# Two transformer blocks in split fp32: up projections by seven products of quarters, hidden activations through DRAM

## The chip, the core and the metric

The kernel runs on one core of a Trainium2 chip. A core has TensorE (matmuls from SBUF into PSUM), VectorE, ScalarE, GpSimd and SyncE, which work through their own queues in order and wait for each other by semaphores, and 16 DMA engines. The metric is the device time of one execution in microseconds, as the median of the runs.

## What is computed

The reference runs two transformer blocks on one sequence of 1024 tokens with 1024 features. The first has a recurrent (RWKV) and convolutional mixer and a gated feed-forward network, the second has two kinds of attention and a squared-ReLU network. The change touches the two networks:

```python
def _channel_mixer(hn, w_up, ffn_conv_w, ffn_conv_b, w_down):      # D_FF = 2816
    f = jnp.einsum('btd,df->btf', hn, w_up)                        # 1024 -> 2 x 2816
    f = _causal_dwconv(f, ffn_conv_w) + ffn_conv_b                 # 3 taps along the sequence
    gate, up = jnp.split(f, 2, axis=-1)
    return jnp.einsum('btf,fd->btd', jax.nn.gelu(gate) * up, w_down)
...
        u = rms_norm(h, g_mlp[i])
        h = h + jnp.square(jax.nn.relu(u @ w_ff1[i])) @ w_ff2[i]   # 1024 -> 4096 -> 1024
```

## The kernel before, in words

Activations are feature-major: a tile has 128 features on the partitions and one half (`hf`, 512 columns) of the sequence. Every fp32 product is made as three matmuls of a faster type: a value is split into a high part (a cast by ScalarE) and a low part (value minus high part, by VectorE or GpSimd), and hi·hi, hi·lo and lo·hi are summed in PSUM. `load_w` (L126) brings a 512 KB block of weights by SyncE's queue (L133), casts it (L134) and subtracts (L135, on the engine that `split_engine` names); `split` (L124, L125) does the same for activations; `mm3` (L138 on) issues 3 x 8 = 24 matmuls of 512 columns for a block of 128 outputs over 1024 inputs and one half; `dense` does it for both halves. Its PSUM tile `ps_mm` comes from three banks in turn (`PBUFS`, mm=3).

The first network (`GatedUp`) has 22 pairs of a gate block j and an up block 22+j. The result of each product goes through ScalarE (L789: bias and middle tap, out of PSUM), two more taps on VectorE (L790, L792, PSUM and SBUF inputs) and small edge operations between the halves; then gelu (L803), the product of gate and up (L806) and a split into tiles that the down projection reads. The second network (`SquaredUp`) has 32 blocks with relu (L826), square (L827) and split. `Ffn` works in chunks of 4 or 5 hidden blocks (`CH1`, `CH2`): the up blocks of a chunk, then `downs`, which adds the chunk's product into eight accumulators in SBUF (L878 copies the first chunk, L880 adds later ones). In the second network the accumulators start from the residual, loaded from `h_d`. The last chunk is woven by `finish`: up blocks of one half, down of the first half, the rest of the up blocks, down of the second, with the norm that follows (sum of squares on TensorE at L205, squares on ScalarE at L232, their additions on VectorE at L234) under them.

The first part of the kernel, up to the first up blocks of half 0, has its TensorE order written by `weave`, which interleaves threads of work by gaps; outside it a scheduler of the language orders each engine's instructions by estimated costs and free buffers. From L1486 the low parts of weights are made on GpSimd, from L1498 on VectorE again, and from L1521 on GpSimd.

## Time and profile before

| what | value |
|---|---|
| median of 3 runs (lowest, highest) | 3130.33 us (3129.96, 3135.51) |
| the profiled execution | 3127.2 us, of it the span 3125.5 us, granted clock 0.971 |
| TensorE busy | 2993.0 us, 96% of the span, 14752 matmuls |
| VectorE, ScalarE, GpSimd busy | 1650.0, 1157.3, 686.8 us |
| DMA | 294.64 MB, mean 94 GB/s |

The busy share is a mean over phases. The mixer lies at 0 to about 830 us, the first network up to about 1500, attention and its branches up to about 2250, the second network and the gate of the last stage behind it. Granted clock 1.00 is the upper of TensorE's two levels, 2.4 GHz. In rows of matmuls the mean duration overlaps from one matmul to the next, so the time per matmul is read from the stretch divided by the count.

### The profile page before, as it was taken

The numbers are of one execution on the slowest core, as the hardware profiler recorded it, in microseconds if no ns is written. First come the engines' busy times: TensorE is split into PE (matmuls) and PEld (weight loads), VectorE is DVE, ScalarE is ACT, GpSimd is POOL, SyncE is SP. The second block draws the span as 40 slices with busy tenths as digits, with TensorE's granted clock in tenths as the row PEclk, the third lists the DMA queues.
The fourth block names the chain that finished last, engine by engine and source line by source line (L and its number), as shares of the span: only waits on it lengthen the run. The fifth ranks groups of instructions, "written<-read, shape, count | busy, mean of one in ns | idle before, by whom it ended". The sixth has DMA issues, their size and how long they took to land.

```text
span 3125.5 us, 39161 instructions
## 1 busy us (share of the span) xinstructions
PE 2993.0 (96%) x14752; PEld 2392.3 (77%) x14752; DVE 1650.0 (53%) x3180; ACT 1157.3 (37%) x2037; POOL 686.8 (22%) x868
## 2 busy tenths in 40 slices
PE   7969899989999999999999999999999999999997
PEld 5747677777788888888778877768888888888876
DVE  6636454537824444535746755576653333333477
ACT  5433332335533232324445655563341221122343
POOL 2143323501100000025633445550000000000343
PEclk8989898999999999999999999999999999999999
DMA  6543422225421111123532312226542111111233
GB/s 216 176 111 103 125 81 83 80 86 171 122 63 48 41 51 51 38 73 123 174 114 68 90 56 70 65 82 210 179 157 59 40 45 55 43 41 48 81 115 134
DMA packets 164860, 294.64 MB, mean 94 GB/s; under 512 B 56120, under 2 KB 65848, under 8 KB 164672
## 3 DMA queue, kind: packets, MB, share of 16 engines
q1 hardware_dynamic: 132400, 241.77, 25.9%
q10 hardware_dynamic: 32272, 50.38, 4.5%
q8 instruction: 116, 1.90, 0.3%
q14 instruction: 72, 0.59, 0.1%
HBM read 238.31 MB, written 53.77 MB: 93 GB/s over the span
## 4 chain that ended last, share of the span: by engine, by line
PE 47%; DVE 3%; ACT 1%; issue 1%; DMA 0%; POOL 0%; ACTq 0%; DVEq 0%; POOLq 0%
PE ps_mm L143 41%; PE pso L1182 1%; PE pss L1137 1%; DVE sq L234 1%; PE pst L1175 1%; PE pss L1136 1%; DVE xl L125 1%; PE pso L1098 0%; DVE xn L257 0%; PE pst L1093 0%; DVE g L1305 0%; PE ps_sp L205 0%; DMA out<-o 0%; PE pss L1066 0%; DVE o L1313 0%
## 5 line engine op out<-in xcount | busy, mean ns | idle before, releaser
L143 PE MATMUL ps_mm<-xh,wh 128*128 128x512 f32 x2304 | 928.3, 403 | 2.9 <-ACT xh L124 1.5
L143 PE MATMUL ps_mm<-xl,wh 128*128 128x512 f32 x2304 | 924.8, 401 | 1.3 <-DVE xl L125 1.3
L135 POOL TENSOR_TENSOR wl<-wr,wh 128x1024 fp32r<-128x1024 f32 (+2 forms) x133 | 279.7, 2105 | 1733.9 <-ACT wh L134 1521.2
L134 ACT CAST wh<-wr 128x1024 fp32r<-128x1024 f32 (+3 forms) x384 | 354.2, 923 | 726.0 <-PE ps_mm L143 648.1
L143 PE MATMUL ps_mm<-xh,wl 128*128 128x512 f32 x2304 | 612.6, 401 | 0.0
L143 PEld LDWEIGHTS ps_mm<-xh,wh 128*128 128x128 f32 x2304 | 439.3, 191 | 103.0 <-issue 2.2
L143 PEld LDWEIGHTS ps_mm<-xl,wh 128*128 128x128 f32 x2304 | 439.4, 191 | 99.6 <-DVE xl L125 2.5
L143 PEld LDWEIGHTS ps_mm<-xh,wl 128*128 128x128 f32 x2304 | 431.0, 190 | 97.3 <-issue 1.9
L135 DVE TENSOR_TENSOR wl<-wr,wh 128x1024 fp32r<-128x1024 f32 (+2 forms) x251 | 273.2, 1089 | 263.9 <-PE ps_mm L143 217.9
L880 DVE TENSOR_TENSOR acc<-acc,ps_mm 128x512 f32<-128x512 f32 x176 | 120.9, 687 | 304.6 <-PE ps_mm L143 304.6
L143 PE MATMUL ps_mm<-hq,wh 128*128 128x512 f32 x864 | 218.6, 395 | 0.0
L143 PEld LDWEIGHTS ps_mm<-hq,wh 128*128 128x128 f32 x864 | 162.8, 188 | 38.0
L143 PE MATMUL ps_mm<-hh,wh 128*128 128x512 f32 x432 | 170.6, 397 | 1.2 <-ACT wh L134 1.2
L143 PE MATMUL ps_mm<-hl,wh 128*128 128x512 f32 x432 | 170.9, 396 | 0.8 <-DVE hl L125 0.8
L657 POOL TENSOR_TENSOR pr<-mt,lt 128x60 f32<-128x60 f32 (+24 forms) x248 | 88.6, 357 | 331.4 <-DMA lt<-d_l 312.6
L1159 POOL TENSOR_SCALAR S<-S,sm 128x512 f32<-128x512 f32 (+3 forms) x96 | 118.8, 1248 | 98.6 <-DVE sm L1157 70.4
L234 DVE TENSOR_TENSOR sq<-sq 128x512 f32<-128x512 f32 x112 | 108.0, 964 | 34.9 <-ACT sq L232 26.4
L790 DVE SCALAR_TENSOR_TENSOR ft<-ps_mm,vec,ft 128x511 f32<-128x511 f32 x88 | 65.7, 746 | 113.1 <-ACT ft L789 112.9
L143 PE MATMUL ps_mm<-hh,wl 128*128 128x512 f32 x432 | 117.0, 397 | 0.0
L143 PE MATMUL ps_mm<-hq,wl 128*128 128x512 f32 x432 | 116.3, 394 | 0.0
L143 PE MATMUL ps_mm<-yh,wh 128*128 128x512 f32 x256 | 103.9, 407 | 5.1 <-ACT yh L124 5.1
L789 ACT ACTIVATE ft<-ps_mm,vec 128x512 f32<-128x512 f32 x88 | 68.5, 779 | 103.2 <-PE ps_mm L143 102.1
(307 smaller groups left out, 4137.8 us busy)
## 6 DMA issues: line engine op xcount, KB each, us to landing
wr<-in_w_up SPq DMA_DIRECT2D x62, 512.0 KB, 3.6
wr<-in_w_in SPq DMA_DIRECT2D x58, 512.0 KB, 3.9
wr<-in_w_ff SPq DMA_DIRECT2D x41, 512.0 KB, 3.6
wr<-in_w_in2g SPq DMA_DIRECT2D x32, 512.0 KB, 3.6
wr<-in_w_ff SPq DMA_DIRECT2D x32, 320.0 KB, 2.9
wr<-in_w_out SPq DMA_DIRECT2D x16, 512.0 KB, 4.3
wr<-in_w_dn SPq DMA_DIRECT2D x32, 256.0 KB, 2.7
res<-h_d SPq DMA_DIRECT2D x32, 256.0 KB, 4.2
```

The source lines that it names most:

```text
L125: (engine or self.nc.vector).tensor_tensor(out=pair[1], in0=src, in1=pair[0], op=ALU.subtract)
L134: nc.scalar.copy(out=hi, in_=raw)
L135: (engine or self.split_engine).tensor_tensor(out=lo, in0=raw, in1=hi, op=ALU.subtract)
L143: self.nc.tensor.matmul(ps, lhsT=a[:, j, :cols], rhs=x[j][hf][part], start=i == 0, stop=i == 3 * kb - 1)
L234: self.nc.vector.tensor_tensor(out=sq, in0=acc, in1=sq, op=ALU.add)
L657: e.tensor_tensor(out=pr, in0=mt[:, :n, i:i + 1].to_broadcast([128, n, m]), in1=lt[:, i:i + 1, i + 1:].to_broadcast([128, n, m]), op=ALU.mult)
L789: nc.scalar.activation(out=t, in_=ps, func=AF.Identity, bias=k.vc("ffn_conv_b", m), scale=c(2))
L790: nc.vector.scalar_tensor_tensor(out=t[:, 1:], in0=ps[:, :-1], scalar=c(1), in1=t[:, 1:], op0=ALU.mult, op1=ALU.add)
L880: k.nc.vector.tensor_tensor(out=o, in0=o, in1=ps, op=ALU.add)
L1136: nc.tensor.matmul(ps, lhsT=qs[:, e, qc], rhs=kh[e][:, kc], start=True, stop=False)
L1137: nc.tensor.matmul(ps, lhsT=qs[own, e, qc], rhs=kl[0][own, kc], start=False, stop=True)
L1159: nc.gpsimd.tensor_scalar(out=s, in0=s, scalar1=sums[0], scalar2=None, op0=ALU.mult)
```

## The change

Up projections of most blocks are made by a Strassen-Winograd scheme with seven products of quarters in place of eight. The quarters are the two halves of the 1024 inputs (4 row tiles each) times two blocks of weights, and the same halves times the two halves of the sequence. In the first network 17 of 22 pairs (gate j and up 22+j, j from 5) go this way, in the second 13 pairs of neighbouring blocks (from block 6). The first 5 and 6 blocks keep `dense`.

`Quads.operands` makes, once per network, the sums and differences of the input: 16 additions of high and low part on GpSimd, 16 differences T1 to T4 on VectorE, and 16 splits. `Quads.weights` makes for every pair four sums or differences S1 to S4 on GpSimd and splits the two raw blocks' quarters (one split of 1024 columns, five of 512; the low parts of S2 and S3 on GpSimd, the rest on VectorE). `pair` issues 7 x 12 matmuls into three PSUM tiles, two of which gather several products (their partial sums are copied out by ScalarE on the way and added by VectorE). The result of a pair goes through the convolution and gelu, or relu and square, as tiles of 1024 columns in SBUF, and is stored in DRAM (`hid_d`) by ScalarE's queue. After all up blocks the down projections read it back and split it (`hidden`), in chunks of 4, 4, 4, 2, 8 and 4 x 6, 8. `finish` only holds the two halves of the last chunk's down projection. Pools in SBUF are opened and closed by phase.

The diff, cut to the parts spoken of:

```diff
-CH1 = (5, 5, 4, 4, 4)
-CH2 = (5, 5, 5, 5, 4, 4, 4)
-BUFS = dict(am=2, q=10, t=32, nt=5, tp=14, tg=5, tr=1, mt=1, pr=2, wc=4, cd=2, sm=10, mk=1)
+CH1 = (4, 4, 4, 2, 8)
+CH2 = (4, 4, 4, 4, 4, 4, 8)
+WORK = dict(nt=5, tg=5, tp=14, am=2)
+MIX = dict(WORK, q=10, tr=1, mt=1, pr=2, wc=4, mk=1, cd=2)
+ATT = dict(WORK, cd=2, sm=10)
+QUAD = dict(T=24, ws=20, ct=5, tg=4)
...
+    def conv(self, m, t, src):
+        k, nc = self.k, self.k.nc
+        c = lambda i: k.vc("ffn_conv_w", i * 2 * self.nff + m)
+        nc.scalar.activation(out=t, in_=src, func=AF.Identity, bias=k.vc("ffn_conv_b", m), scale=c(2))
+        for i in (1, 2):
+            nc.vector.scalar_tensor_tensor(
+                out=t[:, i:], in0=src[:, :-i], scalar=c(2 - i), in1=t[:, i:], op0=ALU.mult, op1=ALU.add)
...
+    def pairs(self, js):
+        return [((j,), j, self.nff + j) for j in js]
+    def pair(self, js, cs, keep):
+        k, j = self.k, js[0]
+        ts = []
+        for part in (0, 1):
+            t = k.a("ct", [128, 1024], name="ft")
+            self.conv(part * self.nff + j, t, cs[part])
+            if part == 0:
+                k.nc.scalar.activation(out=t, in_=t, func=AF.Gelu_apprx_tanh)
+            ts.append(t)
+        k.nc.vector.tensor_tensor(out=ts[1], in0=ts[0], in1=ts[1], op=ALU.mult)
+        keep(j, ts[1])
...
+    def pairs(self, js):
+        return [((j, j + 1), j, j + 1) for j in js[::2]]
+    def pair(self, js, cs, keep):
+        k = self.k
+        for j, c in zip(js, cs):
+            k.nc.scalar.activation(out=c, in_=c, func=AF.Relu)
+            k.nc.vector.tensor_tensor(out=c, in0=c, in1=c, op=ALU.mult)
+            keep(j, c)
...
+    def operands(self, x):
+        k = self.k
+        nc = k.nc
+        half = NB // 2
+        for n, r in (("11", 0), ("21", half)):
+            self.x[n] = [x[r + i][0] for i in range(half)]
+        self.x["22"] = [x[half + i][1] for i in range(half)]
+        for n in ("T1", "T2", "T3", "T4"):
+            self.x[n] = []
+        for i in range(half):
+            raw = {}
+            for n, pr in (("11", x[i][0]), ("12", x[i][1]), ("22", x[half + i][1]), ("21", x[half + i][0])):
+                raw[n] = k.t("r" + n, tag="ws")
+                nc.gpsimd.tensor_tensor(out=raw[n], in0=pr[0], in1=pr[1], op=ALU.add)
+            for n, a, b in (("T1", "12", "11"), ("T3", "22", "12"), ("T2", "22", "T1"), ("T4", "21", "T2")):
+                raw[n] = k.t(n, tag="ws")
+                nc.vector.tensor_tensor(out=raw[n], in0=raw[a], in1=raw[b], op=ALU.subtract)
+                self.x[n].append(k.pair("t" if n == "T4" else "T", n))
+                k.split(raw[n], self.x[n][-1])
+    def weights(self, wd, m0, m1):
+        k = self.k
+        nc = k.nc
+        half = NB // 2
+        a, b = [k.raw_w(wd, m) for m in (m0, m1)]
+        a11, a12, a21, a22 = a[:, :half], a[:, half:], b[:, :half], b[:, half:]
+        ws = lambda n: k.a("ws", [128, half, 128], F32R, n)
+        s1, s2, s3, s4 = [k.a("tg", [128, half, 128], name=f"s{i}") for i in range(1, 5)]
+        for o, x, y, op in ((s1, a21, a22, ALU.add), (s2, s1, a11, ALU.subtract), (s4, a12, s2, ALU.subtract),
+                            (s3, a11, a21, ALU.subtract)):
+            nc.gpsimd.tensor_tensor(out=o, in0=x, in1=y, op=op)
+        ah, al = [k.wp.tile([128, NB, 128], F32R, tag=n, name=n) for n in ("wh", "wl")]
+        k.split(a, (ah, al))
+        w = {"11": (ah[:, :half], al[:, :half]), "12": (ah[:, half:], al[:, half:])}
+        for n, s, e in (("S2", s2, nc.gpsimd), ("S1", s1, nc.vector), ("S3", s3, nc.gpsimd), ("S4", s4, nc.vector),
+                        ("22", a22, nc.vector)):
+            w[n] = ws(n + "h"), ws(n + "l")
+            k.split(s, w[n], e)
+        return w
+    def product(self, ps, w, x, start=True):
+        half = NB // 2
+        terms = [(w[0], j, part) for j in range(half) for part in range(2)] + [(w[1], j, 0) for j in range(half)]
+        for i, (a, j, part) in enumerate(terms):
+            self.k.nc.tensor.matmul(
+                ps, lhsT=a[:, j], rhs=x[j][part], start=start and i == 0, stop=i == 3 * half - 1,
+                skip_group_check=True)
+            yield ROW * H
+    def pair(self, wd, m0, m1):
+        k, x = self.k, self.x
+        nc = k.nc
+        w = self.weights(wd, m0, m1)
+        c0, c1 = [k.a("ct", [128, 1024], name="c") for _ in range(2)]
+        add = lambda o, ps: nc.vector.tensor_tensor(out=o, in0=o, in1=ps, op=ALU.add)
+        o11, o12, o21, o22 = c0[:, hs(0)], c0[:, hs(1)], c1[:, hs(0)], c1[:, hs(1)]
+        px, py, pz = [k.ps("mm", name=n) for n in ("psX", "psY", "psZ")]
+        yield from self.product(px, w["11"], x["11"])
+        nc.scalar.copy(out=o11, in_=px)
+        yield from self.product(py, w["12"], x["21"])
+        add(o11, py)
+        yield from self.product(px, w["S2"], x["T2"], False)
+        nc.scalar.copy(out=o12, in_=px)
+        yield from self.product(pz, w["S1"], x["T1"])
+        nc.scalar.copy(out=o22, in_=pz)
+        yield from self.product(px, w["S3"], x["T3"], False)
+        add(o22, px)
+        yield from self.product(pz, w["S4"], x["22"], False)
+        add(o12, pz)
+        yield from self.product(px, w["22"], x["T4"], False)
+        nc.scalar.copy(out=o21, in_=px)
+        return c0, c1
 class Ffn:
-    def __init__(self, k, up, w_dn, chunks, seed=None):
+    def __init__(self, k, up, w_dn, chunks, name, seed=None):
         self.k, self.up, self.w_dn, self.chunks = k, up, w_dn, chunks
+        self.hid_d = k.dram(name, sum(chunks))
         self.acc = None
         self.seed = seed
         self.hid = {}
@@ -845,32 +977,49 @@
         j0 = sum(self.chunks[:ci])
         return range(j0, j0 + self.chunks[ci])
-    def ups(self, ci, x, hvs=(0, 1), part=slice(None)):
-        for j in self.js(ci)[part]:
-            h = yield from self.up(j, x, hvs)
-            self.hid.setdefault(j, {}).update(h)
+    def ups(self, js, x, hvs=(0, 1)):
+        def keep(j, hf, t):
+            self.k.nc.scalar.dma_start(out=self.hid_d[j][:, hs(hf)], in_=t)
+        for j in js:
+            yield from self.up.blocks(j, x, hvs, keep)
...
+    def quads(self, js, q):
+        def keep(j, t):
+            self.k.nc.scalar.dma_start(out=self.hid_d[j], in_=t)
+        pairs = self.up.pairs(js)
+        for blocks, m0, m1 in pairs:
+            cs = yield from q.pair(self.up.w, m0, m1)
+            if blocks == pairs[-1][0]:
+                self.hidden(0, (0, 1), "ws")
+            self.up.pair(blocks, cs, keep)
     def alloc(self):
         k = self.k
-        acc = []
-        for m in range(NB):
-            if m < 4:
-                if m % 2 == 0:
-                    am = k.a("am", [128, 2, 1024], name="acc")
-                t = am[:, m % 2]
-            else:
-                t = k.q("acc")
-            acc.append(t)
-            if self.seed is not None:
-                k.nc.sync.dma_start(out=t, in_=self.seed[m])
-        self.acc = acc
+        k.a.open("acc", dict(acc=8))
+        self.acc = [k.a("acc", [128, 1024]) for _ in range(NB)]
+        if self.seed is not None:
+            for m in range(NB):
+                k.nc.sync.dma_start(out=self.acc[m], in_=self.seed[m])
+    def hidden(self, ci, hvs, tag="tp"):
+        k = self.k
+        out = self.hid[ci, hvs] = []
+        for j in self.js(ci):
+            out.append({})
+            for hf in hvs:
+                raw = k.load(self.hid_d[j], hf, "h", tag)
+                out[-1][hf] = k.pair(name="h")
+                k.split(raw, out[-1][hf])
...
-    def finish(self, x, then, filler):
+    def finish(self, then, filler):
         ci = len(self.chunks) - 1
         done = set()
         def main():
-            yield from self.ups(ci, x, (0,))
-            yield from self.ups(ci, x, (1,), slice(0, 1))
             yield from self.downs(ci, (0,))
             done.add("down")
-            yield from self.ups(ci, x, (1,), slice(1, None))
-            yield gap(GAP["hid"])
             yield from self.downs(ci, (1,))
             yield from then(1, [t[:, hs(1)] for t in self.acc])
...
+    def ffn(ff, x, first, n):
+        k.a.open("quad", QUAD, "right")
+        q = Quads(k)
+        q.operands(x)
+        run(ff.ups(range(first), x, (1,)))
+        run(ff.quads(range(first, n), q))
+        k.a.close("quad")
+        ff.alloc()
+        k.a.open("att", ATT, "right")
+        for ci in range(len(ff.chunks) - 1):
+            run(ff.downs(ci))
+    ffn(ff1, ff_in, 5, 22)
```

What moves on the engines, at the places that matter. The number behind a name tells one tile from another.

TensorE, first network, the end of one product and the start of the next, before:

```order
L143 MATMUL ps_mm_7901<-xh_7658,wl_7897 128x512
L143 MATMUL ps_mm_7901<-xh_7664,wl_7897 128x512
L143 MATMUL ps_mm_7901<-xh_7670,wl_7897 128x512
L143 MATMUL ps_mm_7943<-xh_7628,wh_7938 128x512 [waits DVE_49,Activation_49]
L143 MATMUL ps_mm_7943<-xl_7629,wh_7938 128x512
L143 MATMUL ps_mm_7943<-xh_7634,wh_7938 128x512
```

The same engine in the changed kernel: the last matmuls of a pair's product 22 (into psX) and the first of the next pair's S1 (into psZ):

```order
L935 MATMUL psX_8473<-T4h_7807,22l_8468 128x512
L935 MATMUL psX_8473<-T4h_7839,22l_8468 128x512
L935 MATMUL psX_8473<-T4h_7871,22l_8468 128x512
L935 MATMUL psX_8473<-T4h_7903,22l_8468 128x512
L935 MATMUL psZ_8618<-T1h_7789,S1h_8598 128x512 [waits Activation_49]
L935 MATMUL psZ_8618<-T1l_7790,S1h_8598 128x512
L935 MATMUL psZ_8618<-T1h_7821,S1h_8598 128x512
```

A product of 24 matmuls into one bank of three has become products of 12, and the seventh of a pair, of which psX is copied at L962, stands directly before the next pair's S1; the other two banks then hold that pair's psX and psY.

ScalarE, first network, about one and a half pairs of blocks before:

```order
L789 ACTIVATE ft<-ps_mm,vec 128x512
L795 COPY edge<-ps_mm 128x2
L803 ACTIVATE ft<-ft 128x512
L134 CAST wh<-wr 128x1024
L789 ACTIVATE ft<-ps_mm,vec 128x512
L803 ACTIVATE ft<-ft 128x512
L789 ACTIVATE ft<-ps_mm,vec 128x512
L795 COPY edge<-ps_mm 128x2
L124 CAST hq<-ft 128x512
```

and between two copies of one pair's result (`c`) in the changed kernel, where `hid_147` is the hidden tensor in DRAM:

```order
L954 COPY c<-psX 128x512
L989 DMA hid_147<-ft 128x1024
L145 CAST S1h<-s_9154 128x512
L145 CAST S3h<-s_9156 128x512
L803 ACTIVATE ft<-c,vec 128x1024
L145 CAST S4h<-s_9157 128x512
L145 CAST wh<-wr 128x1024
L848 ACTIVATE ft<-ft 128x1024
L145 CAST 22h<-wr 128x512
L962 COPY c<-psX 128x512
L803 ACTIVATE ft<-c,vec 128x1024
L950 COPY c<-psX 128x512
```

Between the copies of the fourth-last and of the last product (L954, L962) now stand the store of the pair before, casts of weights of this pair and the next, the first tap (L803) and the gelu (L848).

SyncE's queue, second network, where the last weights of the up blocks and the first of the down blocks are loaded in the changed kernel (`hid_18915` is the hidden tensor, `h_d` the residual):

```order
L157 DMA wr<-in_w_ff 128x1024 x38
L157 DMA wr<-in_w_ff_0 128x512 x2
L140 DMA h<-hid_18915 128x512 x2
L157 DMA wr<-in_w_ff_0 128x512
L140 DMA h<-hid_18915 128x512 x6
L157 DMA wr<-in_w_ff_0 128x512 x2
L1004 DMA acc<-h_d 128x1024 x8
L140 DMA h<-hid_18915 128x512 x14
L157 DMA wr<-in_w_ff_0 128x512 x2
```

The eight accumulator loads, which stood at the first down projection, stand there still, with 22 loads of hidden tiles around them and five of down weights before.

## Rows read from the trace of the kernel before

**Rows 1.** The page of the whole kernel: span, and busy time of each engine.
```profile
span 3125.5 us, 39161 instructions
...
PE 2993.0 (96%) x14752; PEld 2392.3 (77%) x14752; DVE 1650.0 (53%) x3180; ACT 1157.3 (37%) x2037; POOL 686.8 (22%) x868
```

**Rows 2.** Stretches of the span: length, then busy time and instructions of each engine, clock, DMA.
```profile
core 0: us, PE busy (x) PEld busy (x) DVE busy (x) ACT busy (x) POOL busy (x), PEclk, DMA share, GB/s
900.00:1400.00 500.00, 500.00 (x2153) 405.43 (x2152) 207.89 (x321) 140.92 (x214) 14.45 (x6) 1.00 0.17 51
2300.00:2850.00 550.00, 550.00 (x2375) 446.13 (x2374) 197.49 (x278) 124.42 (x179) 0.00 (x0) 1.00 0.18 55
```

**Rows 3.** Groups by line and shape, whole span: count, busy us, mean ns, idle before.
```profile
L134 ACT CAST wh<-wr 128x1024 fp32r<-128x1024 f32 x264 | 276.4, 1047 | 389.8 <-PE ps_mm L143 321.2 <-DMA wr<-in_w_in2g 13.0 <-issue 7.9
...
L135 DVE TENSOR_TENSOR wl<-wr,wh 128x1024 fp32r<-128x1024 f32 x171 | 211.9, 1239 | 180.9 <-PE ps_mm L143 138.1 <-ACT wh L134 27.3 <-issue 4.0
...
L135 POOL TENSOR_TENSOR wl<-wr,wh 128x512 fp32r<-128x512 f32 x32 | 43.2, 1352 | 70.4 <-PE ps_mm L143 57.5 <-ACT wh L134 8.4 <-issue 4.6
L134 ACT CAST wh<-wr 128x512 fp32r<-128x512 f32 x64 | 39.7, 620 | 137.5 <-PE ps_mm L143 128.8 <-DMA wr<-in_w_dn 4.8 <-DMA wr<-in_w_ff 2.1
...
L125 DVE TENSOR_TENSOR hl<-ft,hh 128x512 fp32r<-128x512 f32 x54 | 37.7, 698 | 38.2 <-ACT hh L124 38.2
```

**Rows 4.** Groups by line in 900 to 1400 us, the middle of the first network.
```profile
L789 ACT ACTIVATE ft<-ps_mm,vec 128x512 f32<-128x512 f32 x56 | 43.6, 779 | 83.1 <-PE ps_mm L143 83.1
L790 DVE SCALAR_TENSOR_TENSOR ft<-ps_mm,vec,ft 128x511 f32<-128x511 f32 x56 | 41.9, 748 | 91.6 <-ACT ft L789 91.3
...
L880 DVE TENSOR_TENSOR acc<-acc,ps_mm 128x512 f32<-128x512 f32 x48 | 33.0, 688 | 88.1 <-PE ps_mm L143 88.1
...
L803 ACT ACTIVATE ft<-ft 128x512 f32<-128x512 f32 x28 | 17.7, 634 | 27.1 <-DVE ft L800 27.1
...
L878 ACT COPY acc<-ps_mm 128x512 f32<-128x512 f32 x12 | 7.0, 587 | 19.8 <-PE ps_mm L143 19.6
```

**Rows 5.** Timeline, 1009 to 1013 us: start, length, engine, and the idle time before it.
```profile
1009.64 2.02 PE L143 MATMUL ps_mm<-xh,wl 128*128 128x512 f32 x8
...
1011.49 0.40 PE L143 MATMUL ps_mm<-xh,wh 128*128 128x512 f32 x1
...
1011.69 0.78 ACT L789 ACTIVATE ft<-ps_mm,vec 128x512 f32<-128x512 f32 x1 [1.33 <-PE ps_mm L143]
1011.73 0.40 PE L143 MATMUL ps_mm<-xl,wh 128*128 128x512 f32 x1
...
1012.51 0.75 DVE L790 SCALAR_TENSOR_TENSOR ft<-ps_mm,vec,ft 128x511 f32<-128x511 f32 x1 [1.42 <-ACT ft L789]
```

**Rows 6.** Timeline, 1449.5 to 1456 us, VectorE beside GpSimd.
```profile
1450.10 2.40 POOL L135 TENSOR_TENSOR wl<-wr,wh 128x1024 fp32r<-128x1024 f32 x1 [1.98 <-ACT wh L134]
...
1450.89 2.17 DVE L234 TENSOR_TENSOR sq<-sq 128x512 f32<-128x512 f32 x1 [0.70 <-ACT sq L232]
...
1452.81 2.51 POOL L135 TENSOR_TENSOR wl<-wr,wh 128x1024 fp32r<-128x1024 f32 x1 [0.31 <-ACT wh L134]
...
1452.97 0.68 DVE L880 TENSOR_TENSOR acc<-acc,ps_mm 128x512 f32<-128x512 f32 x1
...
1454.35 1.52 DVE L234 TENSOR_TENSOR sq<-sq 128x512 f32<-128x512 f32 x1 [0.70 <-ACT sq L232]
```

**Rows 7.** DMA issues of the whole span: count, KB each, median us to landing.
```profile
wr<-in_w_up SPq DMA_DIRECT2D x62, 512.0 KB, 3.6
...
h_d<-acc ACTq DMA_DIRECT2D x16, 256.0 KB, 2.0
...
acc<-h_d SPq DMA_DIRECT2D x8, 512.0 KB, 5.5
```

**Rows 8.** TensorE groups by line in 1380 to 1600 us, with their idle time.
```profile
L143 PE MATMUL ps_mm<-hh,wh 128*128 128x512 f32 x32 | 13.2, 419 | 1.2 <-ACT wh L134 1.2
...
L205 PE MATMUL ps_sp<-ones,sq 128*128 128x1 f32 x32 | 4.8, 272 | 6.4 <-DVE ft L800 5.5 <-DVE sq L234 0.9
```

More of the change, by code (lines that the diff above doesn't have):

```diff
@@ L818, in __init__, with blocks @@
         self.k, self.w = k, w
-    def __call__(self, j, x, hvs):
+    def blocks(self, j, x, hvs, keep):
         k = self.k
-        out = {}
         def then(hf, ps):
@@ L1447, in fill @@
         yield has(("norm", 0))
[L1448 removed]
+        yield from ff1.ups(range(5), ff_in, (0,))
     def norm0():
```

116 lines of the change are left out of this document (62 added, 54 removed).

## Prediction

> **What bounds the kernel now.** I read first the busy shares, then the busy time by stretches, then the groups of instructions in one feed-forward stretch, then single instructions in the timeline. The reader is to see that TensorE is busy for 96% of the span [rows 1], and that in the middle of both feed-forward networks it never stops: 500 of 500 us and 550 of 550 us, at a granted clock of 1.00, with VectorE busy for 42% and 36%, ScalarE for 28% and 23%, GpSimd for almost nothing, and the DMA queues for 18% at most [rows 2]. There a matmul costs its slot and nothing else: 500 us over 2153 matmuls is 0.232 us, as is 550 over 2375. So fewer matmuls there is less time, as long as the work that is put in their place stays under them. The other engines are so far from full that this is possible; how closely it is ordered is what decides.
>
> **The pairs.** A pair of hidden blocks over both sequence halves takes 4 products of 24 matmuls now, 96 x 0.232 = 22.3 us. With seven quarter products of 12 it takes 84 x 0.232 = 19.5 us. 17 pairs change in the first network (below: network one) and 13 in the second, so 30 x 12 = 360 matmuls go, 83.5 us. That is the most this change can give through TensorE. The down projections keep their matmuls.
>
> *Network two, per pair.* VectorE gets one split of 1024 columns (1.24 us), three of 512 (0.69 each), three adds from PSUM (0.69) and two squares of 1024 (1.24 each), 7.9 us; GpSimd six operations of 512 columns, at 1.35 us each 8.1 us [rows 3]. ScalarE: one cast of 1024 (1.05), five of 512 (0.62), four copies from PSUM (0.59), two relus of 1024 (about 1.05 each, an estimate from the same growth as the casts), 8.6 us [rows 3, 4]. All have over 10 us of slack in 19.5, and in the new order every product that takes over a PSUM bank starts 12 or more matmuls (2.8 us) after the last one that wrote it, while the copy needs 0.6. I take 19.6 us: 13 x (22.3 - 19.6) = **-35 us**.
>
> *Network one, per pair.* The order of TensorE shows one place with no cover: the product S1 of a pair takes the bank of the product 22 of the pair before, and these stand back to back, since the other two banks hold open sums. S1 waits until the copy of o21 (L962) has emptied the bank. The price is in the timeline: a read by ScalarE starts 0.20 us after the slot that follows the last matmul (1011.49 to 1011.69) [rows 5], a copy of 512 columns takes 0.59 [rows 4], and I add 0.06 for the signal back, an estimate from the 0.04 us between ScalarE's end and VectorE's start (1012.47 to 1012.51) [rows 5]: 0.85 us a pair. The Trainium skill, page Perfetto Trace Analysis, section Optimizing Tensor Performance, says that independent matmul groups should rotate through different PSUM banks so that the evacuation of one overlaps the matmuls of the next; by that the wait would be nil and the sum below 14 us lower. The order does rotate three banks, but with three groups open the rotation comes round too soon, so I go by the rows.
>
> VectorE has more to do here: the same splits and adds, 1.24 + 2.1 + 2.1 us, four convolution taps over 1024 columns (0.75 for 511 [rows 4], about 1.3 each, an estimate by the growth of the splits), and the product of gate and up (1.24): 11.9 us. GpSimd has 8.1 us again. They are not independent: beside a GpSimd subtraction that ran from 1450.10 to 1452.50, a VectorE multiply of two SBUF tiles, 0.69 us when alone, took 2.17 and ended 0.56 us after it; a VectorE add that reads PSUM took its usual 0.68 beside the next one [rows 6]. In network one the taps read SBUF copies now, not PSUM, so 9.8 of the 11.9 us are of the kind that waits, and with GpSimd's 8.1 make 17.9 of 19.5 us. It fits with little to spare, and ScalarE issues in order: the gelu, which waits for the taps, stands two rows ahead of the copy of o21. Bounds: 19.5 us a pair without any wait, 22.3 if every gain is eaten. I take 20.5 (19.5 + 0.85 + 0.15 for some late gelus), since the demand is below the period: 17 x (22.3 - 20.5) = **-30 us**.
>
> **Into the pairs.** Before the first pair 16 sums on GpSimd (21.6 us), 16 differences and 16 splits on VectorE (22 us), and 16 casts on ScalarE must be made from the normalized input. In network one the plain blocks of the second half cover them: ten products of 24 matmuls, 55.7 us, in which VectorE also has the blocks' own conv, product and weight splits, about 7 us for each of five, 35 us; 57 us, some of it stretched by GpSimd as above, and the last four operands (T4) find room only when the plain blocks have read their tiles. The first products of the first pair need no differences (24 matmuls, 5.6 us more of cover). Bounds 0 and 15 us; I take **+5**. In network two only six products (33 us) cover 22 + 6 x 1.9 (square and weight split of a block) + 1.2, some 35 us on VectorE, plus the waits beside GpSimd's 21.6 us: bounds 0 and 20, taken **+8**.
>
> **Out of the pairs.** The hidden blocks are read back from DRAM. All but the last pair's are long there: the trace lands a 256 KB store in 2.0 us and a 512 KB load in 3.6 [rows 7], and a pair comes every 20. Its traffic, 11.5 and 16.8 MB each way per network, is small against 18% of the queues [rows 2]. At the turn, though, the last hidden store waits for VectorE's last product some 6 us after the last matmul, and on ScalarE it stands ahead of the copies that free the banks of the down projections, which gives 3 to 4 us in network one. In network two SyncE's queue holds the loads of the accumulator seeds (5.5 us each when several run together [rows 7]) and of the hidden blocks ahead of most down weights. Bounds 0 and 15 us for each; taken **+4** and **+4**.
>
> **The rest.** A down chunk of two blocks (6 matmuls per product, 1.4 us) leaves VectorE and ScalarE 2.8 us per weight block: **+1**. In the finish no up block mixes with the down projections any more, so the sums of squares of one half can stand under the other half's down matmuls. Now TensorE waits in and around the first network's finish 6.4 us ahead of the column sums, mostly for the convolution's edge, and 1.2 us ahead of down matmuls for a weight cast [rows 8]. Bounds 0 and -8; I take **-5**. The stage before the pairs keeps its order of matmuls and only trades two operand splits for a store.
>
> **The sum.** -35 - 30 + 5 + 8 + 4 + 4 + 1 - 5 = -48. The profiled execution took 3127.2 us, 3.1 below the median of 3130.3; 3127.2 - 48 = 3079, and with half of that difference (the execution is one sample) about **3080 us**.
>
> **Rivals.**
> 1. *Only matmuls count.* The bank wait hides and all entries are covered: 3127 - 83 - 5 = 3039, say 3045 with one entry at 6. For it: 500 busy of 500 us [rows 2] with today's VectorE load. Against it: the back-to-back order above.
> 2. *VectorE and GpSimd bind network one.* Each of nine two-input VectorE instructions a pair waits for part of a GpSimd operation; by [rows 6] one wait adds 0.8 to 1.5 us to an instruction, but GpSimd can't cost more in all than its 8.1 us: 11.9 + 8.1 = 20, plus VectorE's own waits for ScalarE's casts and gelu (1 to 2 us), about 22 us. Network one then gains 17 x 0.3 = 5 us, and the sum is 3079 + 25 = 3104. The Trainium skill, page SBUF — State Buffer, section Who interferes with whom, states the cause as an exclusive lock: the one that issues second fully blocks. The trace agrees with it (2.17 instead of 0.69 us).
> 3. *Slower.* The chain of one pair is serial through in-order queues: S4's end, add (0.69), identity (1.2), two taps (2.6), gelu (1.05), copy of o21 (0.59), then S1. That is 6.1 us against the 38 matmuls (8.8 us) that stand between S4's end and S1. If GpSimd's operations wedge into three of its VectorE steps (3 x 1.3) the chain is 10, TensorE stops for 1.2 us more and the same happens to the weights' splits of the next pair, whose raw sums have one buffer each: 24 us a pair, 17 x 1.7 = +29 in network one. With network two at 20.5 (-23) and entries and turns at 30: 3127 + 29 - 23 + 30 - 5 = 3158. It decides from a mean of 21.7 us over all 30 pairs, where the gain of 0.55 each is what the other terms (+17) take.
> 4. *The matmuls cost more.* The new products change weights as often as the old ones, one load per matmul, so nothing argues for a longer slot; a slot over 0.265 us would be needed (22.3 / 84) to lose all.
>
> **Chances.** My forecast (3062 to 3095) 0.5; rival 1 0.15; rival 2 0.2, with the entries at their upper bounds up to 3118; rival 3 0.13, of which 0.03 ends level; rival 4 0.02. The range 3042 to 3118 leaves about 0.2 out. A measurement of this kernel can tell 0.2% (6 us) from no change. Faster 0.85, within it 0.04, slower 0.11.
>
> **What would show it.** Right: 84 matmuls a pair in 20 to 21 us in network one, with one gap of 0.6 to 0.9 us ahead of each S1 that ends with the copy of L962; 19.5 to 19.7 in network two; gaps of a few us at the first S-products and at the first down projections. Wrong: gaps ahead of the products whose operands VectorE or GpSimd split (S2l, S3l), which is rival 2; VectorE over 90% busy in network one; gelu ending after the last matmul of 22, which is rival 3; or gaps over 15 us where the phases meet.

## The result, and the profile after

The changed kernel takes 3088.8 us in the median of four runs (3081.7 to 3098.4), the kernel before 3132.6 us in the same comparison: a ratio of 0.9862, 95% interval 0.9832 to 0.9892. That is faster by 44 us and lies inside the predicted range; the forecast was 3080. The profiled execution took 3081.7 us, 45.5 below that of the kernel before. It is the fastest of the four, and the four lie in the order of their granted clock: 3081.7 us at 0.971, 3086.9 at 0.968, 3090.7 at 0.965 and 3098.4 at 0.963.

The page of the changed kernel, which answers to [rows 1]:

```profile
span 3079.9 us, 39432 instructions
...
PE 2911.5 (95%) x14392; PEld 2318.3 (75%) x14392; DVE 1813.9 (59%) x3228; ACT 1262.6 (41%) x2187; POOL 1011.8 (33%) x1056
```

360 matmuls are gone, and TensorE's busy time falls by 81.5 us (2993.0 to 2911.5). The span falls by 45.6 only, so 36 us of the gain came back as idle time. To see where, both spans are cut at two instructions that stand in both kernels: the last matmul of the recurrence, and the first score of the attention. The stretches of the kernel before (length, then busy time and instructions of each engine, granted clock, DMA):

```profile
core 0: us, PE busy (x) PEld busy (x) DVE busy (x) ACT busy (x) POOL busy (x), PEclk, DMA share, GB/s
0.00:690.30 690.30, 601.29 (x4063) 467.25 (x4064) 362.40 (x771) 260.62 (x485) 218.72 (x581) 0.90 0.40 118
690.30:1666.60 976.30, 958.30 (x4144) 773.11 (x4141) 512.21 (x800) 356.18 (x537) 161.12 (x86) 0.99 0.28 88
1666.60:3125.50 1458.90, 1433.39 (x6553) 1151.94 (x6551) 775.34 (x1609) 540.53 (x1015) 306.95 (x201) 0.99 0.28 87
```

and of the changed one:

```profile
0.00:692.40 692.40, 596.11 (x4064) 463.05 (x4064) 361.67 (x771) 260.15 (x485) 224.30 (x581) 0.91 0.40 117
692.40:1648.20 955.80, 917.60 (x3941) 732.85 (x3938) 600.25 (x772) 407.96 (x596) 324.73 (x188) 0.99 0.35 112
1648.20:3079.90 1431.70, 1397.82 (x6397) 1122.42 (x6395) 851.98 (x1685) 594.50 (x1106) 462.75 (x287) 0.99 0.35 113
```

The first stretch, in which TensorE's order is the same matmul by matmul, is 2.1 us longer. The second, which holds the first network, is 20.5 us shorter for 204 matmuls less (47 us at the 0.232 of [rows 2]): TensorE idles 38.2 us in it where it idled 18.0, and some 6 us are lost in matmuls that took longer. The third, with the second network, is 27.2 us shorter for 156 matmuls less (36 us), with 33.9 us idle where there were 25.5.

TensorE's groups by line between 885 and 1245 us, the pairs of the first network, with the idle time before each and its releaser (first matmul kind of five of the seven products):

```profile
L935 PE MATMUL psZ<-T1h,S1h 128*128 128x512 f32 x68 | 29.3, 431 | 14.3 <-ACT c L962 14.3
...
L935 PE MATMUL psY<-xh,wh 128*128 128x512 f32 x68 | 27.1, 399 | 2.1 <-DVE c L946 2.1
...
L935 PE MATMUL psX<-T2h,S2h 128*128 128x512 f32 x68 | 26.7, 393 | 0.9 <-ACT c L950 0.5 <-ACT S2h L145 0.4
L935 PE MATMUL psX<-T3h,S3h 128*128 128x512 f32 x68 | 26.7, 393 | 1.4 <-ACT c L954 1.4
...
L935 PE MATMUL psX<-T4h,22h 128*128 128x512 f32 x66 | 26.3, 399 | 0.3 <-DVE c L946 0.3
```

Of the idle time, 14.3 us stand ahead of S1, and all of them end with the copy at L962. In the steady state each of these waits is 0.68 us. One of them in the timeline:

```profile
1063.25 0.86 PE L935 MATMUL psX<-T4h,22l 128*128 128x512 f32 x3
...
1064.15 0.59 ACT L962 COPY c<-psX 128x512 f32<-128x512 f32 x1 [0.32 <-PE psX L935]
...
1064.78 0.50 PE L935 MATMUL psZ<-T1h,S1h 128*128 128x512 f32 x1 [0.68 <-ACT c L962]
```

The third-last matmul starts at 1063.25, the last at 1063.71, so that S1 could have started at 1063.94; it starts at 1064.78, when the copy has ended. With the next slot, which is 0.11 us longer than usual, a pair takes 20.33 us, and thirteen pairs in a row take exactly that. The wait of the third pair is larger, 4.87 us, and the timeline of ScalarE tells why:

```profile
929.12 1.24 ACT L803 ACTIVATE ft<-c,vec 128x1024 f32<-128x1024 f32 x1
936.01 0.62 ACT L145 CAST S2h<-s 128x512 fp32r<-128x512 f32 x1 [5.64 <-POOL s L921]
...
939.10 0.61 ACT L145 CAST S4h<-s 128x512 fp32r<-128x512 f32 x1
939.62 0.58 ACT L962 COPY c<-psX 128x512 f32<-128x512 f32 x1
```

The copy at 939.62 had its matmuls long before. It stands in ScalarE's queue behind the casts S2h to S4h of a later pair, and these wait 5.64 us for GpSimd's sums of weights, of which the first waits for a raw weight block:

```profile
932.77 1.85 POOL L921 TENSOR_TENSOR s<-wr 128x512 f32<-128x512 f32 x1 [5.64 <-DMA wr<-in_w_up]
```

What such a wait costs behind it is told by the granted clock, in the stretch right after it and in the next whole pair:

```profile
940.25:945.50 5.25, 5.25 (x12) 4.14 (x13) 5.25 (x6) 3.03 (x4) 1.67 (x1) 0.50 0.52 181
...
963.12:983.45 20.33, 19.66 (x84) 15.69 (x85) 13.13 (x13) 9.63 (x14) 9.37 (x6) 1.00 0.23 78
```

Twelve matmuls took 5.25 us, 0.44 each, at a granted clock of 0.50 (1.2 GHz), where the pair after them has 0.23 at 1.00 (2.4 GHz): 2.5 us on top of the 4.87.

The second network's pairs and the turn to its down projections, 2290 to 2620 us:

```profile
L935 PE MATMUL psX<-xh,wh 128*128 128x512 f32 x52 | 21.7, 418 | 3.0 <-ACT wh L145 3.0
...
L935 PE MATMUL psX<-T2h,S2h 128*128 128x512 f32 x52 | 20.4, 392 | 2.7 <-ACT S2h L145 2.7
...
L935 PE MATMUL psZ<-T1h,S1h 128*128 128x512 f32 x52 | 20.3, 390 | 0.0
...
L935 PE MATMUL psX<-xh,wl 128*128 128x512 f32 x52 | 16.5, 416 | 2.7 <-DVE wl L146 2.7
...
L165 PE MATMUL ps_mm<-hh,wh 128*128 128x512 f32 x16 | 6.9, 434 | 4.0 <-DVE acc L1029 4.0
```

Here S1 never waits. What is idle is the start of the pairs, 2.7 + 2.7 + 3.0 us for weights and operands, and 4.0 us at the first down projections. From the third pair on two pairs take 38.74 us, 19.37 each. The 4.0 us end with an addition of VectorE, which had waited for its accumulator from DRAM:

```profile
2616.57 1.29 DVE L1029 TENSOR_TENSOR acc<-acc,ps_mm 128x512 f32<-128x512 f32 x2 [5.26 <-DMA acc<-h_d]
```

### The profile page after: what moved, and what is told of

It reads as the page before. It is cut to its first block, busy times and chain, and to the rows that moved or that the text cites. A ratio compares the mean times of both kernels' runs of the same rounds, so it can differ in the third digit from the quotient of the medians.

```text
span 3079.9 us, 39432 instructions
## 1 busy us (share of the span) xinstructions
PE 2911.5 (95%) x14392; PEld 2318.3 (75%) x14392; DVE 1813.9 (59%) x3228; ACT 1262.6 (41%) x2187; POOL 1011.8 (33%) x1056
## 4 chain that ended last, share of the span: by engine, by line
PE 62%; DVE 5%; DMA 2%; issue 2%; ACT 1%; POOL 1%; ACTq 0%; DVEq 0%; SPq 0%; POOLq 0%
PE ps_mm L165 38%; PE psX L935 10%; PE psZ L935 5%; PE psY L935 2%; PE pso L1327 1%; PE pss L1282 1%; PE pst L1320 1%; DVE sq L255 1%; PE pss L1281 1%; POOL s L921 1%; PE pso L1243 0%; DVE wl L146 0%; DVE T L907 0%; PE pst L1238 0%; DVE g L1450 0%
## 5 line engine op out<-in xcount | busy, mean ns | idle before, releaser
L145 ACT CAST wh<-wr 128x1024 fp32r<-128x1024 f32 (+2 forms) x343 | 318.2, 928 | 651.8 <-PE ps_mm L165 532.5
L165 PE MATMUL ps_mm<-xh,wh 128*128 128x512 f32 x1344 | 546.5, 407 | 3.5 <-ACT xh L145 1.7
L165 PE MATMUL ps_mm<-xl,wh 128*128 128x512 f32 x1344 | 543.5, 405 | 1.8 <-DVE xl L146 1.8
L146 POOL TENSOR_TENSOR wl<-wr,wh 128x1024 fp32r<-128x1024 f32 (+1 forms) x109 | 257.0, 2359 | 846.5 <-ACT wh L145 663.2
L165 PE MATMUL ps_mm<-xh,wl 128*128 128x512 f32 x1344 | 369.2, 405 | 0.0
L165 PE MATMUL ps_mm<-hh,wh 128*128 128x512 f32 x864 | 342.9, 397 | 7.8 <-DVE acc L1029 4.0
L165 PE MATMUL ps_mm<-hl,wh 128*128 128x512 f32 x864 | 342.6, 397 | 0.0
L165 PEld LDWEIGHTS ps_mm<-xh,wh 128*128 128x128 f32 x1344 | 256.9, 191 | 61.6 <-issue 3.2
L165 PEld LDWEIGHTS ps_mm<-xl,wh 128*128 128x128 f32 x1344 | 256.9, 191 | 57.4 <-DVE xl L146 2.3
L165 PEld LDWEIGHTS ps_mm<-xh,wl 128*128 128x128 f32 x1344 | 249.7, 191 | 55.2 <-issue 1.9
L165 PEld LDWEIGHTS ps_mm<-hh,wl 128*128 128x128 f32 x864 | 163.7, 190 | 38.2
```

Source lines behind the costliest of these rows:

```text
L145: self.nc.scalar.copy(out=pair[0], in_=src)
L146: (engine or self.nc.vector).tensor_tensor(out=pair[1], in0=src, in1=pair[0], op=ALU.subtract)
L165: self.nc.tensor.matmul(ps, lhsT=a[:, j, :cols], rhs=x[j][hf][part], start=i == 0, stop=i == 3 * kb - 1)
```

## Experiments

Theory: the gain is the matmuls' time, and what is missing of it was lost at four places, each with a cause of its own: the order that puts S1 right behind the bank's last matmul, the start of the pairs in each network, and the turns to the down projections. Rivals: VectorE and GpSimd hold each other up and set the pace of the first network; or the gain comes from the new layout as much as from the products.

The first stretch was between 690.3 and 702.9 us in the eleven profiles, though its matmuls stand in the same order in all; so stretches are compared where a few us matter. The kernel before was timed anew beside each group of runs (medians of 3130.3, 3132.5 and 3127.3 us), so whole kernels are compared by their ratio to it. Each run's second stretch (first network) and third (attention and second network):

| run | ratio to before, 95% interval | 2nd, us | 3rd, us |
|---|---|---|---|
| before | 1 | 976.3 | 1458.9 |
| changed kernel | 0.9862, 0.9832 to 0.9892 | 955.8 | 1431.7 |
| e3_plain | 0.9993, 0.9974 to 1.0012 | 973.1 | 1458.8 |
| e4_ff2 | 0.9939, 0.9919 to 0.9959 | 973.1 | 1435.2 |
| e1_bank | 0.9888, 0.9854 to 0.9923 | 954.5 | 1441.8 |
| e5_order | 0.9834, 0.9810 to 0.9858 | 938.8 | 1437.1 |
| e2_dve | 0.9833, 0.9803 to 0.9862 | 948.8 | 1433.3 |
| e6_order_dve | 0.9770, 0.9752 to 0.9789 | 931.7 | 1436.1 |
| e7_cover | 0.9885, 0.9863 to 0.9908 | 962.3 | 1438.9 |
| e8_order_dve_cover | 0.9762, 0.9740 to 0.9783 | 929.4 | 1426.0 |
| e9_order_dve_sums | 0.9788, 0.9773 to 0.9803 | 933.7 | 1431.5 |

e7's second stretch shows how far such a number goes: its code there is the changed kernel's, its time 6.5 us longer, in an execution with a granted clock of 0.963 where the changed kernel's has 0.971. Each reading below therefore rests on the pairs' period and on single waits, which repeat to the hundredth.

### The layout without the products (e3_plain), and the products in one network (e4_ff2)

```diff
-        run(ff.quads(range(first, n), q))
+        if pairs:
+            run(ff.quads(range(first, n), q))
+        else:
+            run(ff.ups(range(first, n), x))
+            ff.hidden(0, (0, 1), "ws")
```

In e3_plain `pairs` is false for both networks and the operands aren't made; in e4_ff2 it is true for the second.

> Edit: no pairs at all; every up block by the plain three-term product, but the hidden activations still through DRAM, the new pools, chunks and finish. My theory: the layout brings about nothing (4 us at each turn to the down projections lost, about 8 won in the finishes), so the time is that of the kernel before: 3118 to 3130 us, with 14752 matmuls. Rival (the layout itself brings a good part of the gain): under 3112 us.

> Edit: pairs in the second network alone, the first plain as in the run without pairs. My theory: 13 pairs at 19.4 instead of 22.15 us give 36 us, of which the start of the pairs takes back 8.5 us of waits and 3 to 4 us of half clock behind them: 24 us below the run without pairs, 3094 to 3106 us. The first network's share is then the rest, some 20 us less than its matmuls promise (37 us). Rival (the savings of both networks are alike per pair): 13/30 of the whole gain of 44, 19 us or less below the run without pairs.

e3_plain takes 3127.7 us, no different from before. Its two stretches, and those of e4_ff2 in the fence below:

```profile
694.90:1668.00 973.10, 959.98 (x4144) 769.63 (x4139) 513.96 (x808) 352.13 (x529) 138.48 (x70) 0.99 0.34 110
1668.00:3126.80 1458.80, 1435.14 (x6553) 1150.03 (x6551) 776.79 (x1614) 537.81 (x1012) 306.61 (x193) 0.99 0.35 110
```

```profile
692.70:1665.80 973.10, 959.51 (x4143) 769.60 (x4140) 514.21 (x808) 352.07 (x529) 138.40 (x70) 0.99 0.33 110
1665.80:3101.00 1435.20, 1398.92 (x6397) 1123.69 (x6395) 851.45 (x1685) 594.00 (x1106) 463.40 (x287) 0.99 0.34 112
```

The third stretch is 1458.8 us without pairs, as before the change, and 1435.2 with: 23.6 us for the second network's products, where 24 were expected. The changed kernel's second stretch is 17.3 us below e4_ff2's: the first network's share. So the layout, DRAM included, neither brings nor costs anything that these runs show (the interval of e3_plain's ratio is 6 us to either side), and the products bring all of it, the second network more per pair (1.8 us) than the first (1.0). The new finishes are in e3_plain too: TensorE's waits there are those of the changed kernel to 0.2 us, yet the two stretches are only 3.2 and 0.1 us shorter than before.

### More banks (e1_bank), and TensorE's order by hand (e5_order)

```diff
-        px, py, pz = [k.ps("mm", name=n) for n in ("psX", "psY", "psZ")]
+        px, py, pz = [k.ps(t, name=n) for t, n in (("mm", "psX"), ("mm", "psY"), ("sc", "psZ"))]
```

> Edit: the sum psZ of a pair gets its PSUM banks from another tag (two banks that are idle in the feed-forward networks), so that three more banks rotate among psX and psY. My theory: in the first network a pair takes 20.33 us because the product S1 stands right behind the product 22 whose bank it takes over; with another bank the wait of 0.68 us (0.95 us of period) goes, a pair takes 19.4 to 19.5 us, and the kernel gains 14 to 16 us: about 3067 us where the changed kernel has 3082 to 3089. Rival (VectorE and GpSimd, which hold each other up, set the pace of the first network, and the bank wait only hides it): the pairs stay above 20.1 us, with new gaps ahead of products whose operands VectorE or GpSimd split; gain under 4 us.

A miss. The kernel is not faster (0.9888), and the pairs stay at 20.33 us to the hundredth. TensorE's groups of e1_bank between 885 and 1245 us:

```profile
L935 PE MATMUL psX<-xh,wh 128*128 128x512 f32 x68 | 28.4, 417 | 11.3 <-ACT c L962 11.3
...
L935 PE MATMUL psZ<-T1h,S1h 128*128 128x512 f32 x68 | 26.7, 392 | 1.0 <-ACT S1h L145 1.0
...
L935 PE MATMUL psX<-T4h,22h 128*128 128x512 f32 x64 | 25.6, 400 | 2.3 <-DVE c L946 2.3
```

S1 has lost its wait on L962, and psX's first product w11 has it in its place. In the order of this run w11 of a pair stands directly behind 22 of the pair two back, whose bank it takes. The rival explains this no better, since from the fifth pair on no product waits for what VectorE or GpSimd split (the waits in the other two rows shown lie in the first four pairs and the last two). By this order the scheduler issues a product as soon as it may: with more banks it runs one product further ahead, and stands before the next bank. The next run tests that.

```diff
-        run(ff.quads(range(first, n), q))
+        with tc.manual_schedule(engines={mybir.EngineType.PE}):
+            run(ff.quads(range(first, n), q))
```

> Edit: TensorE's order inside the pairs is the program's own (w11, w12, S2, S1, S3, S4, 22 of one pair, then the next pair), not the scheduler's. The run with more banks had kept 20.33 us a pair, with the wait moved from S1 to w11: the scheduler ran one product further ahead and stood before the next bank. My theory: the wait is made by the order, which puts a product directly behind the last one of the bank that it takes over. In the program's order the next psX takes psY's bank, whose last matmul lies 60 matmuls back, and the next psZ takes psX's after 36. Pairs of 19.4 us in the first network, no gap at L962, 14 to 16 us less between the first and the last pair. Rival (a chain of ScalarE and VectorE of about 20.3 us per pair sets the pace, whatever TensorE's order): pairs stay at 20.2 us or more, with gaps elsewhere.

With the three banks of the changed kernel and the program's own order the pairs take 19.37 us. TensorE's groups of e5_order between 990 and 1216 us have no idle time at all, of which two rows:

```profile
L935 PE MATMUL psX<-xh,wh 128*128 128x512 f32 x48 | 19.1, 398 | 0.0
...
L935 PE MATMUL psZ<-T1h,S1h 128*128 128x512 f32 x45 | 17.5, 389 | 0.0
```

and ten pairs in a row (1022.06 to 1215.72) show TensorE busy for the whole stretch:

```profile
1022.06:1215.72 193.66, 193.66 (x841) 157.66 (x840) 128.20 (x121) 97.05 (x132) 85.42 (x53) 1.00 0.26 86
```

The second stretch falls by 17.0 us against the changed kernel, more than the 14 to 16 expected of the pairs, since the waits in the first pairs (7.8 us for 9.5) and at the turn to the down projections (1.8 for 3.8) are shorter too. In the second network, where no such wait stood, the program's order gains nothing: 8.6 us of waits at its start. The interval of the kernel's ratio overlaps that of the changed kernel, so the reading rests on the period. The cause of the 0.68 us is thus shown: not the number of banks, but the order.

### VectorE in place of GpSimd (e2_dve), and both edits (e6_order_dve)

```diff
-            nc.gpsimd.tensor_tensor(out=o, in0=x, in1=y, op=op)
+            nc.vector.tensor_tensor(out=o, in0=x, in1=y, op=op)
...
-        for n, s, e in (("S2", s2, nc.gpsimd), ("S1", s1, nc.vector), ("S3", s3, nc.gpsimd), ("S4", s4, nc.vector),
+        for n, s, e in (("S2", s2, nc.vector), ("S1", s1, nc.vector), ("S3", s3, nc.vector), ("S4", s4, nc.vector),
```

> Edit: the four sums of weights and the low parts of S2 and S3 are made by VectorE instead of GpSimd, in every pair. My theory: nothing waits for GpSimd in the steady state, so the pairs of the first network stay at 20.3 us, with VectorE at about 16 of 20.3 us; only the start changes: the sums of weights come earlier, and the wait of 4.87 us in the third pair, where the copy of o21 is queued behind casts that wait for sums, falls below 2.5 us. Kernel the same within 8 us. Rival (the two engines hold each other up and that sets the pace): the pairs of the first network fall to 20.0 us or less, the second network's stay, kernel 6 us or more faster. Other rival (VectorE becomes the limit): pairs of 21 us and more, gelu late, kernel slower by over 10 us.

Ten pairs of the changed kernel (1003.78 to 1207.12), and ten of e2_dve in the fence below:

```profile
1003.78:1207.12 203.34, 196.59 (x841) 156.91 (x841) 129.77 (x121) 96.08 (x131) 92.98 (x60) 1.00 0.23 78
```

```profile
1013.22:1216.55 203.33, 196.58 (x841) 156.90 (x841) 146.53 (x180) 97.13 (x134) 0.00 (x0) 1.00 0.26 86
```

203.34 and 203.33 us. GpSimd's 93 us of work in them are gone, VectorE has 16.8 us more, and the pace is the same to the hundredth: nothing in the steady state waits for the two engines' contention. VectorE's share of each pair is 12.98 us with GpSimd at work and 14.65 without. What changes is the start: the wait of 4.87 us in the third pair is gone, of the 9.5 us of waits in the first four pairs 1.9 us remain beyond the usual 0.68, and the second stretch is 7.0 us shorter. By the ratios the kernel is 9 us faster, just over the expected 8, but its interval overlaps that of the changed kernel.

> Edit: both the program's order for TensorE in the pairs and VectorE in place of GpSimd for the sums and low parts of weights. My theory: both gains add, 19.4 us a pair and the shorter start of the first network: some 14 us below the run with VectorE alone (3075), 3057 to 3066 us. VectorE is then busy for 16 of 19.4 us in the first network. Rival (VectorE, now without slack, sets the pace): pairs of 20 us and more in the first network, and no gain over the better of the two edits alone.

3060.3 us, as expected, with VectorE at 142.6 of 193.7 us in ten pairs and no idle time of TensorE:

```profile
1011.74:1205.41 193.67, 193.67 (x842) 157.66 (x840) 142.57 (x174) 98.06 (x132) 0.00 (x0) 1.00 0.25 85
```

Both gains add; the interval (0.9752 to 0.9789) lies clear below that of the changed kernel.

### The start of the second network (e7_cover, e8_order_dve_cover, e9_order_dve_sums)

```diff
-    run(ff2.ups(range(6), ff_in2, (0,)))
+    run(ff2.ups(range(8), ff_in2, (0,)))
...
-    ffn(ff2, ff_in2, 6, 32)
+    ffn(ff2, ff_in2, 8, 32)
```

> Edit: eight instead of six blocks of the second network are plain, so that 11 us more of matmuls cover the making of the operands, at the price of one pair (2.8 us). My theory: the waits of 8.5 us at the start of the pairs (and some 3 us at half clock behind them) are VectorE's and GpSimd's operands coming too late; they fall below 3 us, and the second network is 6 to 9 us shorter from the end of the attention to its down projections. Rival (the start waits for the chain of weight loads and sums of the first pairs, not for the operands): the waits stay at 6 us or more and the second network is up to 3 us longer.

Between the two, and a miss for the theory: of the 8.5 us of waits 5.0 are left (0.63, 0.51, 0.14, 3.73), and the stretch from the attention's end to the down projections is 493.2 instead of 494.0 us, with 12 matmuls more in it. The operands were late, and so was something else: the largest wait left is for an addition into c on VectorE.

e8 is e6_order_dve with this edit.

> Edit: the program's order for TensorE, VectorE in place of GpSimd for the weights, and eight plain blocks in the second network instead of six. My theory: what is left at the start of the second network's pairs are 6.2 us of waits for operands, with up to 3.4 us at half clock behind them; with the weights' chain already short, 11 us more of cover takes away both, for 2.8 us of a pair given up. 3 to 7 us faster than with six (3060): 3053 to 3058 us, and no wait over 1 us between the plain blocks and the last pair. Rival (the start is bound by the chain of weights, as the run with the cover alone left 5 us of waits): waits of 3 us or more remain, and the time is 3058 to 3064 us.

In e6_order_dve two waits had remained in this stretch, as TensorE's groups from 2290 to 2590 us show:

```profile
L935 PE MATMUL psX<-T2h,S2h 128*128 128x512 f32 x52 | 21.4, 412 | 4.5 <-ACT S2h L145 4.5
...
L935 PE MATMUL psX<-xh,wl 128*128 128x512 f32 x52 | 14.3, 397 | 1.6 <-DVE wl L146 1.6
```

In e8 TensorE has no idle time from the attention's end to the down projections:

```profile
2098.30:2568.90 470.60, 470.60 (x2046) 382.12 (x2045) 308.73 (x419) 196.61 (x278) 30.79 (x16) 1.00 0.43 143
```

It is 470.6 us against 475.9 in e6, with 12 matmuls more. The kernel takes 3054.9 us, inside the expected range, but by the ratios (0.9762 and 0.9770) it is only 2.5 us faster than e6, where 3 to 7 were expected, and the two intervals overlap, so this step rests on the stretch. With the weights' chain short and the operands covered nothing is left there. This is the fastest version run: 0.9762 of the kernel before, and below the changed kernel beyond both intervals.

In e9 (e6 with one more edit) the 16 sums of high and low parts go to VectorE too:

```diff
-                nc.gpsimd.tensor_tensor(out=raw[n], in0=pr[0], in1=pr[1], op=ALU.add)
+                nc.vector.tensor_tensor(out=raw[n], in0=pr[0], in1=pr[1], op=ALU.add)
```

> Edit: the program's order for TensorE, VectorE in place of GpSimd for the weights, and for the 16 sums of high and low part of the input as well, so that GpSimd does nothing in the networks. In the changed kernel one such sum of GpSimd took 15.93 us at the start of the second network, where others took 1.3 to 2.3, while VectorE ran one instruction with two SBUF inputs after another. Theory: GpSimd gets no turn as long as VectorE's instructions follow without a gap, and the operands wait for that sum, not for the amount of work; without GpSimd VectorE has 11 us more to do, but no operand waits for a sum: waits at the start of the second network below 4 us (6.2 with GpSimd), kernel 3054 to 3060 us. Rival (VectorE's amount of work sets the start): 8 us of waits or more there, 3062 us or more.

A miss for both: 5.54 us of waits in the second network (6.2 before), and a new one of 4.45 us in the first; 3062.3 us. Without GpSimd's late sum VectorE's own amount of work makes the operands nearly as late: up to the 5.54 us it is busy for 33.3 of 35 us, and GpSimd for none.

```profile
2300.00:2335.00 35.00, 29.78 (x128) 23.66 (x126) 33.32 (x52) 16.26 (x26) 0.00 (x0) 0.98 0.32 98
```

So of what was tried, cover is what the start needs, not another division of the work.

## Why the prediction was right

*The pairs of the second network*, 19.6 us forecast, 19.37 measured. The matmul's slot in the pairs is 0.2306 (19.37 / 84), where the plain matmuls before take 0.232 [rows 2]: three of the seven products run in shorter slots (the last section), which the prediction could not know. Against 22.3 us for 96 plain ones the gain is 2.93 a pair, 38 us; forecast 35.

*The pairs of the first network*, 20.5 forecast, 20.33 measured, and for the reason given: one uncovered wait for L962 per pair. It was sized at 0.85 us from [rows 4, 5]; it is 0.96 (20.33 - 19.37). The 0.15 us set aside for late gelus do not exist. The wait stands ahead of 14 of the 17 pairs, the first three having the waits of the start, so the pairs give 17 x 2.93 - 14 x 0.96 = 36 us; forecast 30. The Trainium skill, page Perfetto Trace Analysis, section Optimizing Tensor Performance, has independent matmul groups rotate through different PSUM banks. Here rotation over more banks (e1_bank) did nothing for this wait, while another order over the same three (e5_order) did it all.

*The starts* were the weakest terms. In the first network +5 was forecast, and waits of 9.5 us and 2.5 us at half clock came. The step that failed is the one that counted VectorE's operands against the cover: the operands were nearly in time (0.41 us ahead of the first S2), and the rest came from the second and third pair's weights, a chain of load, sums, casts and splits through two raw buffers that the prediction had not followed, in whose shadow the copy of o21 stood. In the second network +8 was forecast and 8.5 came, before the clock.

*The turns*: +4 and +4 forecast, 3.8 (0.68 ahead of the first down matmul, 3.10 ahead of a later one) and 4.0 measured; the cause in the first, copies behind the last store in ScalarE's queue, was not tried by itself, but ScalarE's timeline shows it. It waits 4.30 us for the last product of gate and up (L850), issues the store, and only then copies the banks out:

```profile
1252.94 0.33 ACTq L989 DMA_DIRECT2D hid<-ft  x1
1253.31 1.56 ACT L1027 COPY acc<-ps_mm 128x512 f32<-128x512 f32 x3 [4.30 <-DVE ft L850]
```

In the second the 4.0 us were the loads of the accumulators (L1004), as the prediction had them in the queue. *The half clock* behind a long wait was not in the sum at all. Besides the 2.5 us of the first start, TensorE runs at 0.50 for 5.7 and 3.4 us behind the two turns and for 2.9 and 3.2 us behind two waits of the second start, which costs about half of these 15.2 us, 7.6 (an estimate). *The finish* took 8.6 us of waits away where 5 were forecast, but partly by luck: around the first network's the waits fell from 7.6 us [rows 8] to 4.2, less than forecast, and from the second network's last chunk to the end of the kernel, which the prediction had left out, from 11.9 to 6.7.

*Rival 1* (only matmuls count, 3045) needed what e8 has, and e8 still stands at 3055. *Rival 2* (the two engines' contention sets the pace) and *rival 3* (the chain of gelu and copy) both fall by e2_dve and e5_order: the same period without GpSimd, and 19.37 us with GpSimd and the other order. VectorE's work, put at 11.9 us a pair, took 12.98 beside GpSimd, not 20 and more; without GpSimd it is about 10.5 (an estimate: the 14.65 of e2 less six operations at 0.69), so the contention is there, at some 2.5 us a pair, and is covered. *Rival 4* falls with the slot. In sum the first start and its clock cost 7 us more than forecast (12 against 5) and the half clock elsewhere 7.6, while the pairs gave 9 more and the finishes 3 to 4, so that the profile ends at 3082 us against 3079 in the working. The mechanism of the pairs was right; that the sum is so close is partly luck, since terms that were off by 7 to 9 us cancel. The median of the runs is 7 us above the profile, with lower granted clocks, and 9 above the forecast.

## What to carry to other kernels

When matmuls are removed from a TensorE that is never idle, the gain here was their slots minus the waits that the new order made; look for the product that follows directly on the last matmul of the bank it takes, since the price (here 0.96 us: the time until the copy starts, the copy of 0.59 us, and a first slot 0.11 us longer) is paid in every round. More buffers did not take this wait away, since the scheduler used them to run further ahead; an order written by hand did. And a new phase pays at its start, for operands and for the first weights through their few buffers, so lay enough old work over it: two more plain blocks took away the 6.2 us of waits that e6 had there and, for 2.8 us of matmuls, made the stretch 5.3 us shorter.

## What the runs showed of the hardware that was not expected

One GpSimd addition of 512 columns took 15.93 us where the shortest took 1.28. Its row (duration in ns: shortest, median, longest of four), and VectorE's timeline from its start at 2322.63 on:

```profile
L904 POOL TENSOR_TENSOR r<-xh,xl x4: 1283/1519/15927, 2322.6 to 2341.0; 128x512 f32<-128x512 f32 x4
```

```profile
2322.46 0.68 DVE L146 TENSOR_TENSOR T3l<-T,T3h 128x512 fp32r<-128x512 f32 x1
2323.07 1.22 DVE L146 TENSOR_TENSOR wl<-wr,wh 128x1024 fp32r<-128x1024 f32 x1
...
2336.10 0.69 DVE L146 TENSOR_TENSOR T3l<-T,T3h 128x512 fp32r<-128x512 f32 x1
2336.70 0.69 DVE L146 TENSOR_TENSOR T2l<-T,T2h 128x512 fp32r<-128x512 f32 x1
2339.84 3.48 DVE L907 TENSOR_TENSOR T<-r,r 128x512 f32<-128x512 f32 x2 [2.44 <-POOL r L904]
```

VectorE ran instructions with two SBUF inputs one behind the other up to 2337.39, each at its usual 0.69 or 1.22 us, and the addition ended at 2338.56, 1.17 us after the last of them. The same 15.93 us stand in the profiles of e2 and e6, where the sums are GpSimd's too; in e7 and e8, with two plain blocks more, the longest such addition is 3.96 us. In [rows 6] the two engines had taken turns instruction by instruction, and I had taken this for the general case; here, as the timeline has it, GpSimd got its turn only when VectorE had nothing ready; no run tried this by itself. The prediction's bound, that GpSimd's work beside VectorE costs a pair at most its own length, holds for VectorE but not the other way round. The Trainium skill, page SBUF — State Buffer, section Who interferes with whom, has the loser wait until the instruction that holds the ports finishes; this wait went on over more than twenty instructions.

The slot of a matmul of 128x512 was not the same for all tiles. One round of e5_order's pairs, from one S2 to the next:

```profile
1058.05 0.39 PE L935 MATMUL psX<-T2h,S2h 128*128 128x512 f32 x1
1066.23 0.40 PE L935 MATMUL psZ<-xh,S4h 128*128 128x512 f32 x1
1077.42 0.39 PE L935 MATMUL psX<-T2h,S2h 128*128 128x512 f32 x1
```

The 36 matmuls of S2, S1 and S3 take 8.18 us, 0.227 each, and the 48 of S4, 22, w11 and w12 take 11.19 us, 0.233 each, at a granted clock of 1.00 and without idle time. The three read T1, T2 and T3, which lie in the pool opened for the pairs, the four read the input and T4, which lie in another; 22 and S4 have their weights in the same tiles as the three. So the slot goes with the tile that the matmul streams in; why, no run here shows.
